# Stacking the weight pools of a one-core encoder layer from the top of SBUF instead of from the bottom

## The chip, the cores and the metric

The kernel runs on one core of a Trainium2 chip. The metric is the device time of one execution in microseconds; the time before is the median of three runs. One further execution was taken by the hardware profiler, and all rows below come from it. Engines are named as the profile names them: PE is the matrix engine (PEld its weight loads), DVE the vector engine, ACT the scalar engine, POOL GpSimd, SP the engine whose queue issues nearly all transfers. Starts and windows are counted from the start of the profiled span.

## What is computed

One layer of a streaming encoder on 512 positions of 2,048 channels in float32:

```python
h = rms_norm(x, pre_mix_g); u, v, g = split(h @ w_in)             # 2048 -> 3 x 1024
y_ssm  = s5_mixer(u, ...)                                         # states, then y * sigmoid(y @ w_glu)
y_conv = silu(layer_norm(causal_depthwise_conv(v * sigmoid(g))))  # 31 taps
x = x + rms_norm(concat(y_ssm, y_conv) @ w_out, post_mix_g)       # 2048 -> 2048
h = rms_norm(x, pre_ffn_g)
gate, val = split(causal_depthwise_conv(h @ w_up, 3 taps))        # 2048 -> 2 x 5632
x = x + rms_norm((gelu(gate) * val) @ w_down, post_ffn_g)         # 5632 -> 2048
```

## The kernel before, in words

Everything is held transposed: channels on the 128 partitions, the 512 positions along the free axis. Every large product goes through `gemm` (lines 100 to 119), which fills four PSUM banks from weight chunks of 128x1024 floats. A chunk is loaded by SP into `wraw` (line 86), and split into a rounded high part `wh` (ACT, line 96) and a remainder `wl` (DVE, line 97). The activations are split in the same way, so that each product needs three matmuls: high times high, low times high, high times low. In a matmul, the 128x128 block of weights is the stationary operand, and the 128x512 activations are the moving operand, streamed past it:

```python
for m in range(4):
    for kk in range(2):
        k = 2 * kc + kk
        xh, xl = rhs[k]
        pe.matmul(ps[m], wh[:, kk, m, :], xh, start=k == 0, stop=False)       # line 116
        pe.matmul(ps[m], wh[:, kk, m, :], xl, start=False, stop=False)        # line 117
        pe.matmul(ps[m], wl[:, kk, m, :], xh, start=False, stop=k == nk - 1)  # line 118
```

There are 8,448 such matmuls, 24 to a chunk, in two families that differ in where the moving operand lies:

- 6,336 whose activations are slices of the four `hl` tiles (128x8x512 each, pool `hl16`): the input projection (6 gemms of 192), the gated linear unit (2 of 96), the output projection (8 of 96), and the first half of the feed-forward part, `up` (22 gemms of 192).
- 2,112 whose activations are the feed-forward part's hidden rows, in `hidh` and `hidl` (pool `hid`, eight buffers of 128x512 each, used in turn): the second half, `down` (11 calls of four gemms of 48).

The program is ordered by a scheduler with priorities. From about 700 us on, the feed-forward part runs as two `up`, one `down`, two `up`, one `down`, and so on; between them ACT and DVE convolve, apply GELU and split the hidden rows (lines 709 to 735), and DVE adds `down`'s PSUM into the accumulators `fa` (line 751, pool `s16`). Ahead of it lie the state-space branch (small matmuls at lines 455, 499, 525 and 526), the convolution branch, which is DVE's (line 567), the output projection and a norm. Behind it lies a norm and the last residual sum (lines 773 to 777).

SBUF is handed out by tile pools. A pool takes its bytes of every partition when it is opened, and pools are stacked: each lies behind the ones opened before it. `const`, `hl16`, `s16`, `wp` (the weights: `wraw`, `wh`, `wl`), `rp` and `t1` are opened at the start and stay open (lines 61 to 70). Behind them `cp`, `p2`, `pp` and `cv` serve the first part and are closed at line 660; `hid` and `t2` (the rows `ab` of the feed-forward convolution) then take their place (lines 663 and 664).

Of the kernel before, what the change touches and what calls it, by code (L numbers as in the profile page):

```python
# [56 lines left out]
def layer_kernel(ctx, tc, a, out):  # L57
# [3 lines left out]
    const = ctx.enter_context(tc.tile_pool(name="const", bufs=1))  # L61
    dram = ctx.enter_context(tc.tile_pool(name="dram", bufs=1, space=bass.MemoryType.DRAM))
    hl16 = ctx.enter_context(tc.tile_pool(name="hl16", bufs=4))
    s16 = ctx.enter_context(tc.tile_pool(name="s16", bufs=2))
    wp = ctx.enter_context(tc.tile_pool(name="wp", bufs=2))
    rp = ctx.enter_context(tc.tile_pool(name="rp", bufs=1))
    psm = ctx.enter_context(tc.tile_pool(name="psm", bufs=6, space=bass.MemoryType.PSUM))
    psa = ctx.enter_context(tc.tile_pool(name="psa", bufs=2, space=bass.MemoryType.PSUM))

    t1 = ctx.enter_context(tc.tile_pool(name="t1", bufs=2))  # L70

    def tmp():
        return t1.tile([P, S], F32, name="tmp", bufs=NTMP)
# [80 lines left out]
    def k4():  # L154
        return cp.tile([P, 1024], F32, name="k4", bufs=3)
# [68 lines left out]
    gpf = cload("post_ffn_g", [P, DK])  # L224
    fcw = cload("ffn_conv_w", [P, 2 * NFF, 3])

    # ---- SSM parameters, states on partitions (group of a pair, state), pairs of groups along the free axis
    uscr = [dram.tile([HC, T, 8, NC], F32, name=f"uscr{m}") for m in range(8)]
    wscr = [dram.tile([2, 16, T, P], F32, name=f"wscr{h}") for h in range(2)]
    bscr = dram.tile([P, 2, NQ, HC], F32, name="bscr")  # L230
# [58 lines left out]
    tt(sh, sh, sh, MUL)  # L289
    ts(sh, sh, -2.0, 1.0, MUL, ADD)  # L290

    # powers of the step: lamr, and lami with the sign turned, by (pair, power)
    lamr = p2.tile([P, NQ, NT], F32, name="lamr")
    lami = p2.tile([P, NQ, NT], F32, name="lami")
    ge.memset(lamr[:, :, 0], 1.0)
# [24 lines left out]
    lpow(1, 2, 2)  # L320
    lpow(1, 3, 4)

    # (step - 1) / eigenvalue
    lr, li = lamr[:, :, 1], sn[:, 0:NQ]
    nr = ts(sm("nr"), lr, -1.0, 1.0, ADD, MUL)
    ab, ab2 = sm("ab"), sm("ab2")
# [20 lines left out]
    tt(tA, tA, tB, SUB)  # L347
    tt(coi, tA, rd, MUL)

    # times powers of the step: columns to rows, and spread over the channels of a group  # L350
    cf = pp.tile([P, 2, NQ, T], F32, name="cf")
    cx = pp.tile([P, NQ, T], F32, name="cx")

# [22 lines left out]
    prep.close()  # L376
    cv = ph1.enter_context(tc.tile_pool(name="cv", bufs=1, reuse_waits="tile"))

    # discretized B
    bsb = k4().rearrange("p (r q h) -> p r q h", r=2, h=HC)  # L380
    bin_ = k4().rearrange("p (r q h) -> p r q h", r=2, h=HC)
    sy.dma_start(out=bin_, in_=a["ssm_b"])
# [12 lines left out]
    for h in range(2):  # L395
# [5 lines left out]
        for mm in range(4):  # L401
# [5 lines left out]
            by = tmp().rearrange("p (q s) -> p q s", q=4)  # L407
# [4 lines left out]
            ve.tensor_tensor(out=w0, in0=w0, in1=bx, op=SUB)  # L412
            ve.tensor_tensor(out=w1, in0=w1, in1=by, op=ADD)

    # C times powers of the step (with the sign of the imaginary part turned)
    for m in range(8):
        ct = cp.tile([P, 2, 4, NT, HC], F32, name="cst", bufs=2)
        cin = p2.tile([P, 2, 4, HC], F32, name="cin")
# [14 lines left out]
            sy.dma_start(out=cscr[m][:, :, gg].rearrange("r p q t -> p r q t"),  # L433
                         in_=ct[PH * gg:PH * gg + PH].rearrange("p r q t h -> p r q (t h)"))

    # ---- input projection: the SSM branch
    def uload(m):
        um = t1.tile([P, S], F32, name="um", bufs=2).rearrange("p (g c) -> p g c", g=8)
        sy.dma_start(out=um, in_=uscr[m].rearrange("h j g c -> (h j) g c"))
        return um  # L440
# [20 lines left out]
    u_evac(pu0, 0)  # L461
    u_evac(gemm(wing[1], xrhs), 4)

    # ---- recurrence over chunks
    ve.memset(st[:, :, :, 0], 0.0)
    lr8 = lam8[:, 0:1, :].broadcast_to([P, 2, NQ])
    for c in range(NC - 1):
# [4 lines left out]
        ve.tensor_tensor(out=sa, in0=sa, in1=st[:, :, :, c + 1], op=ADD)  # L472
        scan_end = ve.tensor_tensor(out=st[:, :, :, c + 1], in0=sa, in1=sx, op=ADD).ins

    # ---- response within a chunk
    kb = s16.tile([P, 4096], F32, name="s16")
    bst = kb[:, 0:1056].rearrange("p (r q h) -> p r q h", r=2, h=HC)
    ge.memset(bst[:, :, NQ, :], 0.0)
# [56 lines left out]
        for i in range(2):  # L535
            sy.dma_start(out=yall[:, m - 1 + i], in_=yscr[m // 2][P * i:P * i + P])

    # ---- input projection: the convolution branch
    csb = cv.tile([P, 8, S], F32, name="csb")

    def vg_evac(ps, i0):
# [28 lines left out]
    for i in range(4):  # L570
        vg_evac(gemm(wing[2 + i], xrhs), 2 * i)

    # ---- SSM branch: operands of the gated linear unit
    yh = hl16.tile([P, 8, S], F32R, name="hl")
    yl = hl16.tile([P, 8, S], F32R, name="hl")
    yc = []
# [4 lines left out]
                         in1=yh[:, m, :].bitcast(F32).rearrange("p (c j) -> p c j", j=T), op=SUB)  # L581
        yc.append(yn)

    # ---- SSM branch: gated linear unit
    zh = hl16.tile([P, 8, S], F32R, name="hl")
    zl = hl16.tile([P, 8, S], F32R, name="hl")
    yrhs = [(yh[:, k, :], yl[:, k, :]) for k in range(8)]
# [10 lines left out]
            se.copy(out=zh[:, m, :], in_=zt)  # L598
            ve.tensor_tensor(out=zl[:, m, :], in0=zt, in1=zh[:, m, :].bitcast(F32), op=SUB)

    # ---- convolution branch: layer norm and swish
    cs = rp.tile([P, S], F32, name="ssq")
    ge.tensor_tensor(out=cs, in0=csb[:, 0], in1=csb[:, 1], op=ADD)
    for i in range(2, 8):
# [21 lines left out]
        se.copy(out=ch[:, i, :], in_=sl)  # L626
        ve.tensor_tensor(out=cl[:, i, :], in0=sl, in1=ch[:, i, :].bitcast(F32), op=SUB)

    # ---- output projection
    yo = [s16.tile([P, 8, S], F32, name="s16") for _ in range(2)]  # L630

    def yt(m):
# [26 lines left out]
    ry = rsqrt_bcast([yss] + last, D, False)  # L659
    ph1.close()  # L660

    # ---- residual, and the norm before the feed-forward part
    hid = ctx.enter_context(tc.tile_pool(name="hid", bufs=8, reuse_waits="tile"))
    t2 = ctx.enter_context(tc.tile_pool(name="t2", bufs=1, reuse_waits="tile"))
    x1scr = dram.tile([P, DK, S], F32, name="x1scr")
# [27 lines left out]
            ge.tensor_tensor(out=xs2, in0=xs2, in1=sq, op=ADD)  # L693
    r2 = rsqrt_bcast([xs2], D)

    # ---- feed-forward part
    fa = [s16.tile([P, 8, S], F32, name="s16") for _ in range(2)]

    def ft(m):
# [150 lines left out]
```

## Time and profile before

| | |
|---|---|
| time, median of 3 runs | 2148.36 us (2146.53 to 2149.66) |
| profiled execution: span from first to last instruction | 2146.2 us |
| PE busy | 2029.9 us, 95% of the span |
| DVE busy | 1215.0 us, 57% |
| ACT busy | 665.7 us, 31% |
| POOL busy | 290.4 us, 14% |
| transfers | 252.36 MB, 118 GB/s in the mean |
| mean granted TensorE clock | 0.972 of full |

The profiled execution is given by its span alone, 2146.2 us; the median of the runs lies 2.2 us above it, which also holds what comes before the first and after the last instruction. A busy time counts the time in which at least one instruction of the engine was under way. Matmuls overlap one another in the records, so that the length of one record (some 390 ns) is not the time that it costs: that is the distance from its start to the start of the next.

### The profile page before, as it was taken

The numbers are of one execution on the slowest core, as the hardware profiler recorded it, in microseconds if no ns is written. First come the engines' busy times: TensorE is split into PE (matmuls) and PEld (weight loads), VectorE is DVE, ScalarE is ACT, GpSimd is POOL, SyncE is SP. The second block draws the span as 40 slices with busy tenths as digits, with TensorE's granted clock in tenths as the row PEclk, the third lists the DMA queues.
The fourth block names the chain that finished last, engine by engine and source line by source line (L and its number), as shares of the span: only waits on it lengthen the run. The fifth ranks groups of instructions, "written<-read, shape, count | busy, mean of one in ns | idle before, by whom it ended". The sixth has DMA issues, their size and how long they took to land.

```text
span 2146.2 us, 23254 instructions
## 1 busy us (share of the span) xinstructions
PE 2029.9 (95%) x9190; PEld 1659.9 (77%) x9190; DVE 1215.0 (57%) x1609; ACT 665.7 (31%) x827; POOL 290.4 (14%) x291
## 2 busy tenths in 40 slices
PE   7767999799997999999999999999999999999995
PEld 6656788677886888888888888888888888888884
DVE  6288999998439552453544535345443464434546
ACT  5111233433535333222312223122231222213233
POOL 6655144303023000000000000000000000000004
PEclk9888999899998999999999999999999999999998
DMA  6785576322423322232223222222232222322242
GB/s 205 170 211 161 202 205 198 95 89 91 174 98 127 109 90 97 98 98 97 91 97 98 98 89 98 98 98 92 96 98 98 98 89 98 98 96 94 95 167 98
DMA packets 111373, 252.36 MB, mean 118 GB/s; under 512 B 28064, under 2 KB 49568, under 8 KB 110752
## 3 DMA queue, kind: packets, MB, share of 16 engines
q1 hardware_dynamic: 106512, 248.77, 36.2%
q10 hardware_dynamic: 4752, 2.11, 0.4%
q8 instruction: 72, 1.18, 0.2%
q14 instruction: 37, 0.30, 0.0%
HBM read 229.67 MB, written 21.17 MB: 117 GB/s over the span
## 4 chain that ended last, share of the span: by engine, by line
PE 72%; DVE 3%; ACT 1%; issue 0%; DVEq 0%; ACTq 0%
PE mm L118 24%; PE mm L116 24%; PE mm L117 24%; DVE hl L685 0%; DVE s L775 0%; DVE s L682 0%; DVE wl L97 0%; DVE hidh L683 0%; PE aux L144 0%; DVE s L776 0%; DVE hidl L683 0%; ACT L137 0%; ACT wh L96 0%; ACT tmp L759 0%; ACT tmp L655 0%
## 5 line engine op out<-in xcount | busy, mean ns | idle before, releaser
L97 DVE TENSOR_TENSOR wl<-wraw,wh 128x1024 fp32r<-128x1024 f32 (+1 forms) x353 | 441.3, 1250 | 777.7 <-ACT wh L96 771.7
L116 PE MATMUL mm<-hl,wh 128*128 128x512 f32 x2112 | 831.9, 395 | 15.2 <-ACT wh L96 9.4
L118 PE MATMUL mm<-hl,wl 128*128 128x512 f32 x2112 | 778.6, 397 | 60.2 <-DVE wl L97 60.2
L117 PE MATMUL mm<-hl,wh 128*128 128x512 f32 x2112 | 831.4, 394 | 0.2 <-DVE hl L685 0.2
L96 ACT CAST wh<-wraw 128x1024 fp32r<-128x1024 f32 (+1 forms) x353 | 370.4, 1050 | 1091.3 <-PE mm L117 1004.7
L118 PEld LDWEIGHTS mm<-hl,wl 128*128 128x128 f32 x2112 | 403.5, 191 | 154.9 <-DVE wl L97 70.1
L116 PEld LDWEIGHTS mm<-hl,wh 128*128 128x128 f32 x2112 | 402.7, 191 | 99.8 <-ACT wh L96 9.8
L117 PEld LDWEIGHTS mm<-hl,wh 128*128 128x128 f32 x2112 | 402.5, 191 | 86.6 <-DVE hl L685 1.4
L117 PE MATMUL mm<-hidl,wh 128*128 128x512 f32 x704 | 277.6, 394 | 0.0
L116 PE MATMUL mm<-hidh,wh 128*128 128x512 f32 x704 | 277.4, 395 | 0.0
L118 PE MATMUL mm<-hidh,wl 128*128 128x512 f32 x704 | 256.6, 395 | 0.0
L761 POOL TENSOR_TENSOR ssq<-ssq,tmp 128x512 f32<-128x512 f32 x11 | 17.3, 1577 | 1394.2 <-ACT tmp L759 1393.7
L567 DVE SCALAR_TENSOR_TENSOR csb<-z,c_conv_w,csb 128x512 f32<-128x512 f32 x210 | 182.9, 930 | 0.0
L116 PEld LDWEIGHTS mm<-hidh,wh 128*128 128x128 f32 x704 | 132.2, 188 | 32.6 <-ACT wh L96 0.5
L118 PEld LDWEIGHTS mm<-hidh,wl 128*128 128x128 f32 x704 | 132.2, 188 | 32.0
L117 PEld LDWEIGHTS mm<-hidl,wh 128*128 128x128 f32 x704 | 132.2, 188 | 31.6
L751 DVE TENSOR_TENSOR s<-mm,s 128x512 f32<-128x512 f32 x160 | 109.9, 691 | 51.1 <-PE mm L118 50.6
L726 DVE SCALAR_TENSOR_TENSOR tmp<-ab,c_ffn_conv_w,tmp 128x512 f32<-128x512 f32 x176 | 125.5, 748 | 0.0
L724 ACT ACTIVATE tmp<-ab,c_ffn_conv_w 128x512 f32<-128x512 f32 x88 | 63.0, 720 | 44.5 <-DVE ab L716 44.5
L716 DVE TENSOR_TENSOR ab<-mm,rr 128x512 f32<-128x512 f32 x88 | 60.4, 689 | 8.2 <-PE mm L118 4.5
L564 POOL TENSOR_TENSOR csb<-csb,pt 128x512 f32<-128x512 f32 x30 | 54.0, 1800 | 53.6 <-ACT pt L563 53.6
L732 ACT CAST hidh<-tmp 128x512 fp32r<-128x512 f32 x44 | 27.2, 621 | 76.6 <-DVE tmp L730 76.6
(212 smaller groups left out, 964.6 us busy)
## 6 DMA issues: line engine op xcount, KB each, us to landing
wraw<-in_ffn_w_up SPq DMA_DIRECT2D x176, 512.0 KB, 3.4
wraw<-in_ffn_w_down SPq DMA_DIRECT2D x88, 512.0 KB, 3.4
wraw<-in_w_in SPq DMA_DIRECT2D x47, 512.0 KB, 5.0
wraw<-in_w_out SPq DMA_DIRECT2D x32, 512.0 KB, 3.4
cst<-cscr SPq DMA_DIRECT2D x16, 576.0 KB, 5.0
cscr<-cst SPq DMA_DIRECT2D x16, 288.0 KB, 4.4
k<-in_ssm_bT SPq DMA_DIRECT2D x8, 512.0 KB, 3.7
um<-uscr SPq DMA_DIRECT2D x16, 256.0 KB, 5.0
```

Source lines behind the costliest of these rows:

```text
L96: se.copy(out=h[:, o], in_=raw[:, o])
L97: ve.tensor_tensor(out=l[:, o], in0=raw[:, o], in1=h[:, o].bitcast(F32), op=SUB)
L116: pe.matmul(ps[m], wh[:, kk, m, :], xh, start=k == 0, stop=False)
L117: pe.matmul(ps[m], wh[:, kk, m, :], xl, start=False, stop=False)
L118: pe.matmul(ps[m], wl[:, kk, m, :], xh, start=False, stop=k == nk - 1)
L564: ge.tensor_tensor(out=csb[:, c, :], in0=csb[:, c, :], in1=pt, op=ADD)
L567: ve.scalar_tensor_tensor(out=csb[:, c, :], in0=zk, scalar=w, in1=csb[:, c, :], op0=MUL, op1=ADD)
L716: ve.tensor_tensor(out=t[:, 2:], in0=ps[j], in1=r2, op=MUL)
L724: se.activation(out=o, in_=t[:, 0:S], func=AF.Copy, scale=fcw[:, c, 0:1])
L726: ve.scalar_tensor_tensor(out=o, in0=t[:, k:k + S], scalar=fcw[:, c, k:k + 1], in1=o, op0=MUL, op1=ADD)
L732: se.copy(out=h, in_=cvt[0])
L751: ve.tensor_tensor(out=ft(m), in0=ps[i], in1=ft(m), op=ADD)
```

## The change

Four pools are opened with `side="right"`: they are stacked from the top of SBUF downwards, in the order in which they are opened. The other pools stay at the bottom and close up. Nothing else differs but some comment lines, which are emptied.

```diff
     hl16 = ctx.enter_context(tc.tile_pool(name="hl16", bufs=4))
-    s16 = ctx.enter_context(tc.tile_pool(name="s16", bufs=2))
-    wp = ctx.enter_context(tc.tile_pool(name="wp", bufs=2))
-    rp = ctx.enter_context(tc.tile_pool(name="rp", bufs=1))
+    s16 = ctx.enter_context(tc.tile_pool(name="s16", side="right", bufs=2))
+    wp = ctx.enter_context(tc.tile_pool(name="wp", side="right", bufs=2))
+    rp = ctx.enter_context(tc.tile_pool(name="rp", side="right", bufs=1))
...
-    t1 = ctx.enter_context(tc.tile_pool(name="t1", bufs=2))
+    t1 = ctx.enter_context(tc.tile_pool(name="t1", side="right", bufs=2))
```

The two built programs hold the same 13,705 instructions in the same order on every engine, with the same operands and the same waits. What differs is the place of the tiles, in bytes of each partition:

| tiles | before | after |
|---|---|---|
| `hl` (moving operand of 6,336 matmuls) | 20,320 to 85,856 | the same |
| `hidh`, then `hidl` (moving operand of 2,112) | 170,976 to 203,744 | 85,856 to 118,624 |
| `wh`, `wl` (stationary operand of all 8,448) | 130,912 to 147,296 | 180,192 to 196,576 |
| `wraw` | 118,624 to 130,912 | 167,904 to 180,192 |
| `s16` (accumulators; in the first part states and responses) | 85,856 to 118,624 | 196,576 to 229,344 |
| `rp` | 147,296 to 151,392 | 163,808 to 167,904 |
| `t1` (`tmp`, `evt`, `um` and others) | 151,392 to 170,976 | 144,224 to 163,808 |
| `ab` | 203,744 to 216,200 | 118,624 to 131,080 |
| `k4` of `cp` | 170,976 to 183,264 | 85,856 to 98,144 |
| `cst` of `cp` | 183,264 to 192,480 | 98,144 to 107,360 |
| `csb` of `cv` | 197,920 to 214,304 | 112,800 to 129,184 |
| `z` of `cv` | 214,304 to 225,176 | 129,184 to 140,056 |

## Rows read from the trace of the kernel before

**Rows 1.** The page: span, busy time, the span in 40 slices.

```profile
span 2146.2 us, 23254 instructions
...
PE 2029.9 (95%) x9190; PEld 1659.9 (77%) x9190; DVE 1215.0 (57%) x1609; ACT 665.7 (31%) x827; POOL 290.4 (14%) x291
...
PE   7767999799997999999999999999999999999995
...
PEclk9888999899998999999999999999999999999998
```

**Rows 2.** Stretches: length, busy us (instructions) by engine, granted clock, DMA share, GB/s.

```profile
core 0: us, PE busy (x) PEld busy (x) DVE busy (x) ACT busy (x) POOL busy (x), PEclk, DMA share, GB/s
...
200.00:300.00 100.00, 94.55 (x506) 75.71 (x505) 95.71 (x267) 29.36 (x35) 18.88 (x16) 0.93 0.64 199
300.00:400.00 100.00, 87.47 (x466) 75.33 (x465) 100.00 (x105) 40.30 (x51) 46.17 (x29) 0.90 0.65 180
400.00:500.00 100.00, 93.37 (x395) 74.35 (x394) 100.00 (x123) 35.60 (x46) 15.72 (x8) 0.98 0.28 91
...
799.70:2119.50 1319.80, 1319.78 (x5761) 1081.24 (x5760) 600.51 (x716) 374.42 (x441) 17.34 (x11) 1.00 0.29 98
```

**Rows 3.** PE in order of time: start us, record's length us, line, operands.

```profile
930.62 0.39 PE L117 MATMUL mm<-hl,wh 128*128 128x512 f32 x1
930.85 0.39 PE L118 MATMUL mm<-hl,wl 128*128 128x512 f32 x1
931.07 0.39 PE L116 MATMUL mm<-hl,wh 128*128 128x512 f32 x1
931.30 0.39 PE L117 MATMUL mm<-hl,wh 128*128 128x512 f32 x1
931.53 0.39 PE L118 MATMUL mm<-hl,wl 128*128 128x512 f32 x1
931.75 0.40 PE L116 MATMUL mm<-hidh,wh 128*128 128x512 f32 x1
931.99 0.39 PE L117 MATMUL mm<-hidl,wh 128*128 128x512 f32 x1
932.21 0.40 PE L116 MATMUL mm<-hidh,wh 128*128 128x512 f32 x1
932.45 0.39 PE L117 MATMUL mm<-hidl,wh 128*128 128x512 f32 x1
...
976.32 0.39 PE L118 MATMUL mm<-hidh,wl 128*128 128x512 f32 x1
976.55 0.39 PE L116 MATMUL mm<-hl,wh 128*128 128x512 f32 x1
...
1063.60 0.40 PE L116 MATMUL mm<-hidh,wh 128*128 128x512 f32 x1
```

**Rows 4.** PE by line from 799.7 to 2119.5 us: count, busy us, mean ns, idle before.

```profile
L117 PE MATMUL mm<-hl,wh 128*128 128x512 f32 x1217 | 473.5, 389 | 0.0
L116 PE MATMUL mm<-hl,wh 128*128 128x512 f32 x1216 | 473.1, 389 | 0.0
L118 PE MATMUL mm<-hl,wl 128*128 128x512 f32 x1217 | 442.9, 389 | 0.0
L117 PE MATMUL mm<-hidl,wh 128*128 128x512 f32 x704 | 277.6, 394 | 0.0
L116 PE MATMUL mm<-hidh,wh 128*128 128x512 f32 x704 | 277.4, 395 | 0.0
L118 PE MATMUL mm<-hidh,wl 128*128 128x512 f32 x703 | 256.2, 395 | 0.0
```

**Rows 5.** Waits from 709 to 2119 us: us in total, times, longest.

```profile
ACT wh L96 <- PE mm L117: 809.2, 237, 4.5
DVE wl L97 <- ACT wh L96: 698.9, 201, 4.4
...
SPq L86 <- DVE wl L97: 1284.4, 253, 7.9
```

**Rows 6.** Small matmuls on `um`: duration ns min/median/max, first and last start.

```profile
L455 PEld LDWEIGHTS aux<-um,s x128: 132/138/232, 120.0 to 139.6; 128*64 128x64 f32 x128
L455 PE MATMUL aux<-um,s x128: 222/222/366, 120.0 to 139.7; 128*64 128x64 f32 x128
L455 PEld LDWEIGHTS aux<-um,csb x128: 132/138/138, 159.3 to 176.0; 128*64 128x64 f32 x128
L455 PE MATMUL aux<-um,csb x128: 222/222/270, 159.3 to 176.0; 128*64 128x64 f32 x128
```

**Rows 7.** PE in order of time, lines 525 and 526.

```profile
393.13 0.39 PE L525 MATMUL aux<-um,k 128*128 128x64 f32 x2
393.35 0.39 PE L526 MATMUL aux<-tmp,cst 128*128 128x64 f32 x2
393.57 0.39 PE L525 MATMUL aux<-um,k 128*128 128x64 f32 x2
393.80 0.39 PE L526 MATMUL aux<-tmp,cst 128*128 128x64 f32 x2
```

**Rows 8.** Instructions of DVE and ACT by form: count, busy us, mean ns.

```profile
L734 DVE TENSOR_TENSOR hidl<-tmp,hidh 128x512 fp32r<-128x512 f32 x44 | 30.2, 689 | 9.3 <-ACT hidh L732 9.3
...
L732 ACT CAST hidh<-tmp 128x512 fp32r<-128x512 f32 x44 | 27.2, 621 | 76.6 <-DVE tmp L730 76.6
...
L599 DVE TENSOR_TENSOR hl<-tmp,hl 128x512 fp32r<-128x512 f32 x8 | 5.5, 687 | 0.0
...
L626 ACT CAST hl<-tmp 128x512 fp32r<-128x512 f32 x8 | 4.7, 620 | 0.0
```

## Prediction, made before the changed kernel ran

> **What bounds the kernel now.** I read the page first, then the stretches, then PE's instructions one by one, then the waits. On the page [rows 1] PE is busy for 95% of the span, and in the 40 slices its row stands at 9 from about a third of the span to the last slice, with the granted clock at 9 or more. [...] The waits say the same from the other side [rows 5]: ACT, before it may overwrite a `wh` buffer, stood 809.2 us behind PE's matmuls of line 117, and DVE waited for ACT; SP's queue stood 1284.4 us behind the split that frees a `wraw` buffer. Weights are ready early and wait for PE, so a faster PE has all that it needs, and each nanosecond taken from a matmul there comes off the end.
>
> The change adds and removes no instruction and no wait, so the question is whether any instruction's speed depends on where its operands lie. For this the length of a record is the wrong measure; the distance between starts is the right one. In order of time [rows 3] PE's starts can be followed across the border between `up` and `down`. Ahead of 931.75 us, where the moving operand is `hl`, starts lie 0.22 to 0.23 us apart; behind it, where it is `hidh` or `hidl`, they lie 0.22 and 0.24 us apart by turns. Over whole calls, where rounding does not matter: the `down` that starts at 931.75 us ends where `hl` comes back at 976.55 us, which is 44.80 us for 4 gemms of 48 = 192 matmuls, 233.3 ns each. The two `up` from there to 1063.60 us take 87.05 us for 384 matmuls, 226.7 ns each. **A matmul that streams from `hid` costs 6.6 ns more than one that streams from `hl`.**
>
> What could cause that other than the place? The form is the same, 128x128 stationary and 128x512 moving [rows 3]; so are the weight tiles `wh` and `wl`, the PSUM pool and the clock. No wait of PE stands beside either family, as the idle time before each group is 0.0 [rows 4], the extra time runs through the whole of the call, and it falls on all three lines alike, as the mean records show: 394 and 395 ns against 389. The operands are contiguous rows of 512 floats in both. What remains is the place: `hl` lies at 20,320 to 85,856 bytes, `hid` at 170,976 to 203,744.
>
> **The change part by part.**
>
> *Hidden rows down (`hid`).* They go to 85,856 to 118,624, straight behind `hl`. If they then stream like `hl`, each of 2,112 matmuls saves 233.3 - 226.7 = 6.6 ns. The count is 11 calls of 192, and 704 + 704 + 703 = 2,111 of them are recorded [rows 4] in the stretch that PE fills. Together that is 2,112 x 6.6 ns = **13.9 us**, or 1.27 us a call. None of it lies beside longer work, as PE never pauses there. Next in line after PE would be DVE with 600.51 of 1319.80 us, far off. This term is between 0 (place plays no part) and 13.9 us; I take 13.9, because the new place borders on the fast rows and is far from the slow ones.
>
> *Weights up (`wp`).* `wh` and `wl` go from 130,912 to 180,192 and above. No row shows a large matmul with weights that high, so I bound the cost. From below: no gain beyond what `hl` shows. From above: if a stationary operand above some place cost what a moving one does, 6.6 ns on each matmul. The nearest rows are the small ones. At line 455 the same `um` streams past blocks of `s16` (85,856 and above) and of `csb` (197,920 and above): loads take 138 ns at the median and matmuls 222 ns in both groups [rows 6]. At lines 525 and 526 the stationary operand is `k4` (170,976 to 183,264) and `cst` (183,264 to 192,480), and pairs start every 0.22 to 0.23 us whichever it is [rows 7]. So a load shows no price for its place up to 214,304 bytes, and I take 0. The upper end stays as a rival below.
>
> *Accumulators, temporaries, `ab`, convolution rows.* DVE and ACT now read and write elsewhere. The subtraction that makes `hidl` from tiles all above 151,392 takes 689 ns, and the one that reads and writes `hl` takes 687; ACT's casts take 621 into `hidh` and 620 into `hl` [rows 8]. That is at most 2 ns for the place. Where DVE is the limit, in the convolution from 200 to 500 us, it runs 267 + 105 + 123 = 495 instructions [rows 2], so 1.0 us to either side at 2 ns each. I take 0. In the feed-forward part these instructions are covered by PE, and even a tenth more on DVE's 600.51 us would stay covered.
>
> *Everything ahead of 700 us.* All its large matmuls stream from `hl`, which does not move. I take 0.
>
> The sum is -13.9 us against the profiled span of 2146.2 us, thus 2132.3 us. The median of the runs stands 2.2 us above that span, so the forecast is 2148.4 - 13.9 = **2134.5 us**, 0.65% faster.
>
> [...]
>
> **The rivals.**
>
> 1. *Only part of the hidden rows gets fast.* What the trace fixes is that 85,856 and below is fast and 170,976 and above slow; a border may lie anywhere between, and the new `hid` reaches up to 118,624. If it is at half of the 229,344 bytes in use, 114,672, the last two of eight `hidl` buffers stay slow: 10 of the 44 hidden rows at 16 matmuls each, 160 x 6.6 ns = 1.1 us lost of the gain, 2135.5 us. If it is at 98,304, all of `hidl` (704) and two of eight `hidh` buffers (10 rows x 32 = 320) stay slow: the gain is 1,088 x 6.6 ns = 7.2 us, 2141.2 us. For it speaks that no row lies between; against it, that most of the gap is above 118,624.
>
> 2. *Nothing changes*, 2148.4 us: the 6.6 ns belong to something that `down` has apart from the place, its shorter sums of four blocks or the eviction after every 48 matmuls. Against it: `down`'s extra time is spread over all its matmuls, and evictions come in a few places. For it speaks only that I cannot see the place itself in a row.
>
> 3. *Slower.* The price belongs to the higher operand of the two, moving or stationary, and sets in between 147,296 (the end of `wl`, which is fast) and 170,976. Then weights from 180,192 on make every matmul slow: `hid` gains nothing, and the 4,224 matmuls of `up` lose 6.6 ns each, 27.9 us, and with the other 2,112 on `hl`, at most another 13.9 us where PE is the limit. That gives 2176 to 2190 us. It decides as soon as weights above 170,976 cost a long matmul anything. Rows 6 and 7 speak against it, though with short matmuls.
>
> **How the numbers follow.** The full or nearly full gain (2134.5, or 2135.5 with the border at half) has 0.80: the difference is in the rows, uniform, on the engine that sets the end. The other partial cases have 0.10, no change 0.06, slower 0.04. A measurement of this kernel tells about 0.2%, 4.3 us, from no change. Faster by more than that takes the 0.80 and most of the partial cases: 0.89; within 0.2%: the 0.06 and the rest, 0.07; slower 0.04. The range reaches from 2132 (the 1.0 us of DVE, and the spread of the runs, 2146.5 to 2149.7) to 2142 (the border at 98,304).
>
> **What would show it.** In the profile after, the distance between starts in `down` should be 226.7 ns and a call should take 43.5 us instead of 44.8, with `up` unchanged at 87.05 us for two. The stretch from the first to the last `down` should be 13.9 us shorter, and the stretches ahead of 700 us alike within a microsecond or two. Rival 1 would show some matmuls of `down` at 233 ns, by buffers; rival 2, all of them; rival 3, `up` at 233 ns as well. The prediction is wrong if `down` keeps its 44.8 us, or if it gains and another stretch gives the gain back.

## The result, and the profile after

The changed kernel takes 2174.55 us (median of 4 runs, 2174.14 to 2174.81) against 2147.45 us before (4 runs, 2146.05 to 2149.66). The ratio is 1.0122, with a 95% interval of 1.0108 to 1.0136: 1.2% slower, where 0.65% faster was forecast.

The page of the changed kernel, the same sections as in [rows 1]:

```profile
span 2172.4 us, 23254 instructions
...
PE 2060.9 (95%) x9190; PEld 1664.3 (77%) x9190; DVE 1216.1 (56%) x1609; ACT 664.8 (31%) x827; POOL 287.1 (13%) x291
...
PE   7767989799998999999999999999999999999995
...
PEclk9878999999998999999999999999999999999998
```

PE has 31.0 us more of busy time for the same 9,190 matmuls (2060.9 against 2029.9). DVE, ACT and POOL are within 4 us of what they were, and the mean granted clock is 0.974 in place of 0.972. That speaks against a new wait, and the stretches settle it. Here is the stretch that PE fills, from the first `down` on, to be read beside the last row of [rows 2] (stretch, busy us and instructions by engine, clock, DMA share, GB/s):

```profile
806.99:2145.70 1338.71, 1338.67 (x5760) 1085.69 (x5759) 601.38 (x716) 373.45 (x441) 17.33 (x11) 1.00 0.29 96
```

It is still full to 0.04 us, at a granted clock of 1.00, and 18.9 us longer. PE in order of time at the borders between `up` and `down`, as in [rows 3] (start us, length of the record, line, operands):

```profile
940.84 0.40 PE L116 MATMUL mm<-hidh,wh 128*128 128x512 f32 x1
...
985.46 0.39 PE L116 MATMUL mm<-hl,wh 128*128 128x512 f32 x1
...
1074.70 0.40 PE L116 MATMUL mm<-hidh,wh 128*128 128x512 f32 x1
```

A `down` takes 985.46 - 940.84 = 44.62 us for 192 matmuls, 232.4 ns each; it took 233.3. The two `up` behind it take 89.24 us for 384, 232.4 ns each; they took 226.7. **`down` stayed slow, and `up` became slow as well.** The sum closes on the span. Two `up` cost 2.19 us more, and there are nine and a half such pairs behind the first `down`: 20.8 us. Ten `down` gain 0.18 us each, and the last loses 0.1: -1.7 us. Ahead of the first `down`, which starts at 806.99 us in place of 799.9, 7.1 us are lost. Together that is 26.2 us, and 2172.4 - 2146.2 is 26.2. Of the 7.1 us, 4.7 lie ahead of the first `up`, which starts at 661.51 us in place of 656.82, and 2.4 in the three `up` behind it, which would owe 576 x 5.7 ns = 3.3 us if PE never paused there. Of the 4.7 us, the output projection owes at most 768 x 5.7 ns = 4.4. The 1,344 matmuls on `hl` ahead of it would owe 7.7 us more; PE is not full there (87.47 of the 100 us from 300 us on [rows 2]), and little of that can show.

### The profile page after: what moved, and what is told of

It is laid out like the page before. It is cut to its first block, busy times and chain, and to the rows that moved or that the text cites. A ratio compares the mean times of both kernels' runs of the same rounds, so it can differ in the third digit from the quotient of the medians.

```text
span 2172.4 us, 23254 instructions
## 1 busy us (share of the span) xinstructions
PE 2060.9 (95%) x9190; PEld 1664.3 (77%) x9190; DVE 1216.1 (56%) x1609; ACT 664.8 (31%) x827; POOL 287.1 (13%) x291
## 4 chain that ended last, share of the span: by engine, by line
PE 72%; DVE 3%; ACT 0%; issue 0%; DVEq 0%; ACTq 0%
PE mm L118 24%; PE mm L116 24%; PE mm L117 24%; DVE hl L685 0%; DVE s L775 0%; DVE s L682 0%; DVE hidh L683 0%; DVE wl L97 0%; PE aux L144 0%; DVE s L776 0%; DVE hidl L683 0%; ACT L137 0%; ACT tmp L759 0%; ACT tmp L655 0%; ACT s L658 0%
## 5 line engine op out<-in xcount | busy, mean ns | idle before, releaser
L116 PE MATMUL mm<-hl,wh 128*128 128x512 f32 x2112 | 844.8, 401 | 21.2 <-ACT wh L96 12.7
L117 PE MATMUL mm<-hl,wh 128*128 128x512 f32 x2112 | 843.9, 400 | 0.2 <-DVE hl L685 0.2
L118 PE MATMUL mm<-hl,wl 128*128 128x512 f32 x2112 | 789.2, 402 | 53.5 <-DVE wl L97 53.3
```

## The experiments

The forecast's border of place is one theory. The third rival, a border that counts for the weights too, is near in its number (2176 to 2190 us), so the runs had to tell whether any border exists. A second theory came from the table of places. Modulo 256 bytes, `hl` and the weights both stood at 96 before and `hid` at 224; after, the weights stand at 224 and both activations at 96. So the slow family is each time the one whose moving operand starts half a period of 256 bytes away from the weights. The third theory is that each operand's own place modulo 256 counts. The paddings of runs 2 to 4 are placed so that the other tiles stay or move by 2,048 bytes, except that `wraw` moves by 128 bytes with the weights in run 2, and `s16` and `wraw` do so in run 4. In the other runs, what lies behind a padding moves along with it. The instructions, their order and their waits are those of before unless the text says otherwise.

**1. `hid` of the kernel before, 128 bytes higher** (`hid_128_up`).

```diff
+    ctx.enter_context(tc.tile_pool(name="pada", bufs=1)).tile([P, 32], F32, name="pada")
     hid = ctx.enter_context(tc.tile_pool(name="hid", bufs=8, reuse_waits="tile"))
```

> The kernel before with 128 bytes of padding ahead of the pool hid, so that hidh and hidl start at 171,104 in place of 170,976; hl and the weights stay. Theory place (a border somewhere between 147,296 and 170,976 above which either operand costs more): no change, down stays at 233.3 ns a matmul, up at 226.7, time 2147.5. Theory distance (what counts is the start of the moving operand less that of the weights, modulo 256: 0 is fast, 128 is slow; before, hl and weights both stand at 96 modulo 256 and hid at 224): hid now stands at 96, down falls to 226.7 ns, time 2133.6. Theory own place modulo 256 (96 fast, 224 slow, for each operand by itself): the same as distance.

**2. The weights of the changed kernel, 128 bytes lower** (`right_weights_128_down`): a padding of 32 floats from the top ahead of `wp`, and one of 480 floats behind it.

> The changed kernel with 128 bytes of padding above the weight pool and 1,920 below it, so that wh starts at 180,064 in place of 180,192 (96 in place of 224 modulo 256); hl and hid stay at 96. Theory place: no change, up and down at 232.4 ns, 2174.5. Theories distance and own place modulo 256: up and down both at 226.7 ns; against before the 2,112 matmuls of down gain 6.6 ns each, so about 2133.6.

**3. The weights of the kernel before, 128 bytes higher** (`weights_128_up`): a tile of 32 floats in `wp` between `wraw` and `wh`, and 480 floats ahead of `rp`.

> The kernel before with 128 bytes of padding between wraw and wh and 1,920 behind wl: the weights stand at 224 modulo 256, hl at 96, hid at 224 (hid moves up by 2,048 as a whole). Theory place: no change, up 226.7 ns, down 233.3, 2147.5. Theory distance: up becomes slow (232 to 233 ns), down fast (226.7): about 2147.5 + 27 - 14 = 2161. Theory own place modulo 256: up and down both slow, about 2175.

**4. `hl` and the weights of the kernel before, 128 bytes higher** (`hl_weights_128_up`): 32 floats ahead of `hl16`, 480 ahead of `rp`.

> The kernel before with 128 bytes of padding ahead of hl and 1,920 behind wl: hl, wh and wl all stand at 224 modulo 256, and hid, moved by 2,048 as a whole, at 224 too. Theory place: no change, up 226.7 ns, down 233.3, 2147.5. Theory distance: everything fast, up and down at 226.7 ns, about 2133.6. Theory own place modulo 256: everything slow, 232 to 233 ns, about 2175.

The times of the four are of one execution each, with the kernel before at 2147.98 us on the same chip; the first two rows are the medians given above:

| | `hl`, weights, `hid` modulo 256 | distance in `up` / `down` | `up` ns | `down` ns | time, us |
|---|---|---|---|---|---|
| before | 96, 96, 224 | 0 / 128 | 226.7 | 233.3 | 2147.45 |
| after | 96, 224, 96 | 128 / 128 | 232.4 | 232.4 | 2174.55 |
| `hid_128_up` | 96, 96, 96 | 0 / 0 | 226.7 | 226.7 | 2136.40 |
| `right_weights_128_down` | 96, 96, 96 | 0 / 0 | 226.7 | 226.7 | 2136.44 |
| `weights_128_up` | 96, 224, 224 | 128 / 0 | 233.3 | 226.8 | 2166.58 |
| `hl_weights_128_up` | 224, 224, 224 | 0 / 0 | 226.7 | 226.7 | 2137.71 |

The nanoseconds are worked out from three starts of each run, as above. Those of `hid_128_up` (PE in order of time):

```profile
932.71 0.39 PE L116 MATMUL mm<-hidh,wh 128*128 128x512 f32 x1
...
976.23 0.39 PE L116 MATMUL mm<-hl,wh 128*128 128x512 f32 x1
...
1063.27 0.39 PE L116 MATMUL mm<-hidh,wh 128*128 128x512 f32 x1
```

those of `right_weights_128_down`:

```profile
932.73 0.39 PE L116 MATMUL mm<-hidh,wh 128*128 128x512 f32 x1
...
976.25 0.39 PE L116 MATMUL mm<-hl,wh 128*128 128x512 f32 x1
...
1063.29 0.39 PE L116 MATMUL mm<-hidh,wh 128*128 128x512 f32 x1
```

those of `weights_128_up`:

```profile
941.07 0.39 PE L116 MATMUL mm<-hidh,wh 128*128 128x512 f32 x1
...
984.61 0.40 PE L116 MATMUL mm<-hl,wh 128*128 128x512 f32 x1
...
1074.20 0.39 PE L116 MATMUL mm<-hidh,wh 128*128 128x512 f32 x1
```

and those of `hl_weights_128_up`:

```profile
933.63 0.39 PE L116 MATMUL mm<-hidh,wh 128*128 128x512 f32 x1
...
977.15 0.39 PE L116 MATMUL mm<-hl,wh 128*128 128x512 f32 x1
...
1064.19 0.39 PE L116 MATMUL mm<-hidh,wh 128*128 128x512 f32 x1
```

In the first, `down` takes 43.52 us and the two `up` 87.04: all fast, with `hid` as high in SBUF as ever; the second, the changed kernel with its weights still at the top, is the same to 10 ns, and so is the fourth. In the third, `down` takes 43.54 us and the two `up` 89.59: the two families have changed places, and no tile changed the part of SBUF that it lies in. Place falls with all four runs. Own place falls with the fourth, where everything stands at 224 and everything is fast, and with the third, where `hid` at 224 is fast. The distance theory foretold every pair of nanoseconds to within 0.3 ns of its values or ranges; for the third run's time it gave 2161 us, since I left out that the output projection pays as well (768 x 6.6 ns = 5.1 us). Since 157 x 256 bytes (`hid` less `wh` in the first) and 432 x 256 (`wh` less `hl` before) both cost 226.7 ns a matmul, an odd number of periods was as good as an even one: the period that these runs show is 256 bytes or a part of it.

Runs 1, 2 and 4 lie 2.8 to 4.1 us above the 2133.6 that the theory gave. In the trace of run 1 the stretch from the first `down` to the end is 13.8 us shorter than before, as worked out, but that `down` starts at 802.15 us in place of 799.9, though nothing streams from `hid` ahead of it. In the nine traces of this case in which `up` is fast, this start lies between 797.9 and 803.1 us, so that 2 us there tell nothing of the edit; the 7.1 us above are no better known than that.

**5 and 6. Other distances** (`hid_32_64_96_160`, `all_32_up_hid_192_224_0_128`). The hidden buffers stand in four groups a to d with paddings between. A `down` then reads a and b by turns, or c and d, 24 matmuls each; the order of the instructions is that of before, but the buffers have other names and some waits differ. In the second of the two, `hl` and the weights are also 32 bytes higher.

```diff
-    hid = ctx.enter_context(tc.tile_pool(name="hid", bufs=8, reuse_waits="tile"))
+    hid = ctx.enter_context(tc.tile_pool(name="hid", bufs=2, reuse_waits="tile"))
...
-            h = hid.tile([P, S], F32R, name="hidh")
+            h = hid.tile([P, S], F32R, name="hidh" + "abcd"[i % 4])
```

> The kernel before, where the eight hidden buffers stand in four groups (a to d, two buffers of hidh and two of hidl each, used in turn by four up calls) with padding between, so that hid less weights is 32, 64, 96 and 160 modulo 256; hl and weights stay at distance 0. [...] Theory distance as an alignment (only multiples of 128 or 64 are special): 64 or 32 is either as fast as 0 or as slow as 128, nothing between. If some distance is better than 0, its groups fall under 226.7 ns. With all four slow, 2147 us; with all four fast, 2134.

> As the run before it, but hl and the weights both 32 bytes higher (at 128 modulo 256, distance 0 still), and the four groups of hid at distance 192, 224, 0 and 128. If only the distance counts: up stays at 226.7 ns, group c (0) at 226.7, group d (128) at 233; a and b as their mirror images 64 and 32 if the price has no sign. If an operand's own place modulo 64 or 128 counts as well, up departs from 226.7 ns, either way.

PE in order of time, the first of the two runs; each row is the first matmul of 24 on one group:

```profile
933.23 0.40 PE L116 MATMUL mm<-hidhc,wh 128*128 128x512 f32 x1
...
938.85 0.39 PE L116 MATMUL mm<-hidhd,wh 128*128 128x512 f32 x1
...
944.47 0.40 PE L116 MATMUL mm<-hidhc,wh 128*128 128x512 f32 x1
...
1065.23 0.40 PE L116 MATMUL mm<-hidha,wh 128*128 128x512 f32 x1
...
1070.83 0.40 PE L116 MATMUL mm<-hidhb,wh 128*128 128x512 f32 x1
...
1076.34 0.40 PE L116 MATMUL mm<-hidha,wh 128*128 128x512 f32 x1
```

and the second:

```profile
929.66 0.39 PE L116 MATMUL mm<-hidhc,wh 128*128 128x512 f32 x1
...
935.10 0.40 PE L116 MATMUL mm<-hidhd,wh 128*128 128x512 f32 x1
...
940.69 0.39 PE L116 MATMUL mm<-hidhc,wh 128*128 128x512 f32 x1
...
1060.89 0.39 PE L116 MATMUL mm<-hidha,wh 128*128 128x512 f32 x1
...
1066.49 0.40 PE L116 MATMUL mm<-hidhb,wh 128*128 128x512 f32 x1
...
1072.08 0.39 PE L116 MATMUL mm<-hidha,wh 128*128 128x512 f32 x1
```

A twenty-fourth of each difference, by distance modulo 256 (some 0.4 ns rough, as the starts are shown to 10 ns):

| distance | 0 | 32 | 64 | 96 | 128 | 160 | 192 | 224 |
|---|---|---|---|---|---|---|---|---|
| ns a matmul | 226.7 | 233.3 | 229.6 | 234.2 | 232.9 | 234.2 | 233.3 | 232.9 |

Of the eight only 0 is fast. 64 pays less than half of the price (229.6 ns; its later turns lie at 229 too), and 192, its mirror image, pays all of it (233.3), so the price depends here on which of the two operands lies ahead. It is not the all or nothing that an alignment would give, nor a smooth hill with its top at 128. As 128 bytes is slow (232.9 ns), the period in these runs is 256 bytes itself and no part of it. `up` of the second run keeps 226.7 ns with everything 32 bytes higher: here too the distance counts, and not a tile's own place. No distance beats 0. The runs took 2148.44 and 2142.78 us in one execution each, beside 2150.61 for the kernel before.

**7 to 9. Whose distance counts?** A matmul streams its activations while the weights of the one behind it are being loaded; two rows of loads further down show it. First only `wl` is put out of step (`wl_128_up`), then only `hidl` (`hidl_128_up`), then `wl` again with the last two matmuls of each three exchanged (`wl_128_up_second`).

```diff
+        "wl" in seen or wp.tile([P, 32], F32, name="pada", bufs=1); seen.add("wl")
         l = wp.tile([P, 1024], F32R, name="wl")
...
-                    pe.matmul(ps[m], wh[:, kk, m, :], xl, start=False, stop=False)
-                    pe.matmul(ps[m], wl[:, kk, m, :], xh, start=False, stop=k == nk - 1)
+                    pe.matmul(ps[m], wl[:, kk, m, :], xh, start=False, stop=False)
+                    pe.matmul(ps[m], wh[:, kk, m, :], xl, start=False, stop=k == nk - 1)
```

> The kernel before with 128 bytes of padding between wh and wl: wh stays at 96 modulo 256, wl, and with it hid, stand 128 higher: wl at 224, hid at 96, hl at 96. Theory own pair (a matmul pays for the distance of its own two operands): of each three matmuls the one of line 118 (wl) is slow, those of lines 116 and 117 fast, in up and down. Theory next load (a matmul pays while it streams for the distance of the weights that are loaded beside it, those of the matmul behind it): the one of line 117 is slow, as wl is loaded beside it. Either way a mean of 226.7 + 6.6 / 3 = 228.9 ns in both, about 2147.5 + 10 - 9 = 2148.5.

> hidh at distance 0 from all weights, hidl at 128. Lines 116 and 118 (hidh) fast, line 117 (hidl) slow by 6.6 ns, whichever weights count, a mean of 228.9 ns in down, if each matmul pays for itself; the run with wl moved gave 231.6 instead, so if mixed distances disturb their neighbours, 230 to 232 ns with all three lines above 226.7. up stays at 226.7.

> The run wl_128_up (wl alone 128 bytes out of step) with the last two matmuls of each three exchanged: high weights by high part, low weights by high part (line 117 now), high weights by low part (line 118 now). Theory own pair: the matmul that uses wl, now line 117, shows the largest distance to the next start. Theory next load: the matmul ahead of it, line 116, beside whose stream wl is loaded, shows the largest. If both count, 116 and 117 both stand some 6 ns above 226.7 and 118 near it, a mean of 231 ns as before the exchange.

PE in order of time in `hidl_128_up`:

```profile
946.32 0.39 PE L118 MATMUL mm<-hidh,wl 128*128 128x512 f32 x1
946.55 0.39 PE L116 MATMUL mm<-hidh,wh 128*128 128x512 f32 x1
946.77 0.40 PE L117 MATMUL mm<-hidl,wh 128*128 128x512 f32 x1
947.01 0.39 PE L118 MATMUL mm<-hidh,wl 128*128 128x512 f32 x1
947.23 0.39 PE L116 MATMUL mm<-hidh,wh 128*128 128x512 f32 x1
```

Here each matmul pays for itself. From the start of line 117, the one on `hidl`, to the next start it is 234.2 ns in the mean; from lines 116 and 118 it is 226 to 227. `down` comes to 228.9 ns a matmul, as a third of the price gives, and `up` keeps 226.7; the time was 2140.77 us in one execution, with the kernel before at 2148.5.

With `wl` out of step, both expectations of a single payer failed: `up` and `down` stood at 231.6 ns, not 228.9, and the time was 2166.56 us, with the kernel before at 2150.61. The exchanged order tells who pays (matmuls in order of time in `wl_128_up_second`, then the loads for the last two of them):

```profile
1002.16 0.39 PE L118 MATMUL mm<-hl,wh 128*128 128x512 f32 x1
1002.39 1.08 PE L116 MATMUL mm<-hl,wh 128*128 128x512 f32 x4
1003.30 0.40 PE L117 MATMUL mm<-hl,wl 128*128 128x512 f32 x1
1003.54 0.39 PE L118 MATMUL mm<-hl,wh 128*128 128x512 f32 x1
1003.76 0.40 PE L116 MATMUL mm<-hl,wh 128*128 128x512 f32 x1
1004.00 0.40 PE L117 MATMUL mm<-hl,wl 128*128 128x512 f32 x1
```

```profile
1003.54 0.19 PEld L116 LDWEIGHTS mm<-hl,wh 128*128 128x128 f32 x1
1003.77 0.19 PEld L117 LDWEIGHTS mm<-hl,wl 128*128 128x128 f32 x1
```

The `wl` of the matmul that starts at 1004.00 us is loaded from 1003.77 us on, beside the stream of the matmul that starts at 1003.76.

Over all `up` of this run from 800 us on, the mean from a matmul on `wh` to the next start is 226.7 ns if that next one uses `wh` too (1,208 recorded pairs) and 232.5 ns if it uses `wl` (1,220 pairs), though it streams from the same `hl` tiles. So the weights that are loaded beside the stream count. The matmul that uses `wl` itself shows 234.2 ns, although `wh` is loaded beside it. Both neighbours of a load out of step pay, 5.8 and 7.5 ns; a third of their sum on top of 226.7 is 231.1, and 231.1 is what `up` and `down` measure. In `wl_128_up` the single distances in `up` are spread from 226 to 241 ns, and the mean of 231.6 is not put together from these two prices. A stream out of step cost its own matmul 7.5 ns in `hidl_128_up` and the next one nothing (226); a block of weights out of step cost two matmuls 13.3 ns together. The time was 2163.43 us, with the kernel before at 2151.52. What is not told apart is whether the matmul on `wl` pays for its own weights or because the load ahead of it ended late.

**10 and 11. The two repaired kernels, timed.** The first is run 1, the second run 2; each was run four times, and the kernel before seven times beside them.

> The kernel before with hid 128 bytes higher, timed. By distance, the FFN gains 2,112 x 6.6 ns = 13.9 us and the part ahead of 700 us stays: about 2133.6 to 2136.5, 0.5 to 0.65% faster than before, and some 1.8% faster than the changed kernel (2174.55).

> The changed kernel with its weights 128 bytes lower, timed. By distance the same as the run before it, within 0.1%: with all distances at multiples of 256 the side of SBUF on which a pool lies is worth nothing. By a theory of place (streamed tiles low, weights high) it would be faster than that run.

The kernel before with `hid` 128 bytes higher took 2137.66 us (2132.72 to 2138.84), a ratio of 0.9946 (0.9930 to 0.9962) to before. The changed kernel with its weights 128 bytes lower took 2135.12 us (2133.44 to 2137.65), 0.9938 (0.9922 to 0.9955). Both beat both kernels: 0.5 to 0.6% below before and 1.7 to 1.8% below the change. The first lies 1.2 us above the range that I had given for it (2133.6 to 2136.5), and the two medians 0.12% apart, where I had given 0.1%. But their intervals overlap widely, so no worth of the side of SBUF is measured, neither for streamed tiles in the lower half nor for weights in the upper.

## Why the prediction was wrong

- **What bounds the kernel** held. PE fills the feed-forward part before (last row of [rows 2]) and after (1338.67 of 1338.71 us), no other engine came near it (DVE, the next, was busy for 601.38 us after), and the 6.6 ns between the families before were real and lay on the path. Runs 1 and 2 gain 11.6 and 11.5 us in one execution each (2147.98 to 2136.40 and 2136.44), 10.8 and 13.4 us in runs 10 and 11, where 13.9 had been worked out; the kernel before itself ran from 2145.57 to 2151.28 us there.
- **The step that failed** is "What remains is the place". I ruled out form, waits and clock rightly, and then read the two families' addresses as high and low. The same table of places holds the starts modulo 256, and there the families differ as well. Runs 1 to 4 show that the distance between the moving operand and the weights, modulo 256 bytes, decides which family is slow, and the part of SBUF does not.
- **The term for `hid`** (13.9 us) failed through that step. The change did bring `hid` in step with `hl`, but it moved the weights half a period away from both. `down` was out of step before and after, and gained 0.9 ns a matmul in place of 6.6.
- **The term for the weights** (0) was bounded by rows that could not bear it. The matmuls of [rows 6] stand at distances of 128 and 192, so neither is the fast case. Those of [rows 7] do stand at 0 in line 525 (`um` less `k4`), and in line 526 at 64, 0, 192 and 128 by turns (`tmp` less the rows of `cst`, which are 576 bytes long), and are equally fast: a pair starts every 0.22 to 0.23 us in both, so that with these 64 columns the price does not show. The nearest rows in place were not the nearest in kind. What this term measured is 5.7 ns on each of the 4,224 matmuls of `up`, 24 us, and up to 4.4 us in the output projection, which I had put at nothing along with all else ahead of 700 us.
- **Rival 3** came within 2 us of the time (2174.55 against 2176 at its lower end) by a mechanism that runs 1 to 4 exclude; that it came near was luck. Its chance of 0.04 was too small for another reason as well: a difference that I could place only by one pair of families had two operands in it, and the change moved both.
- **Rival 1**'s borders and **rival 2**'s shorter sums are out: the `down` of run 1 has the same sums and evictions, and is as fast as `up`, 226.7 ns a matmul in both.

## What to carry to other kernels

Where two families of the same instruction differ by a few nanoseconds on the engine that sets the end, write down every operand's start, and look at it modulo small powers of two before reading it as a place. A padding of 128 bytes is a cheap test of such a reading, and here it was worth 0.5% of the kernel. When pools are moved, the moving operands and the weights of long float32r matmuls should be kept at the same start modulo 256 bytes (here 226.7 ns a matmul, and 229.6 to 234.2 at the seven other distances tried), and the distance between starts in the trace, not the length of a record, tells whether they are.

## What the runs showed that I had not expected

In these runs a 128x512 matmul with a 128x128 load beside it cost 226.7 ns when its moving operand and the weights around it started a multiple of 256 bytes apart, and 229 to 234 ns at the other seven multiples of 32, 64 being the mildest (229.6). Why a distance costs anything, no run shows. Open are also why 64 is milder than 192 (233.3), and why a distance of 128 costs 233.3 ns a matmul in the `down` of before and the `up` of `weights_128_up`, 232.9 in group d and 232.4 in the changed kernel: the `up` of `weights_128_up` and that of the changed kernel have the same two starts modulo 256 and still differ by 0.9 ns, so something besides the distance counts a little.
